# Hybrid retention and attention block on one Trainium2 core: merged branches by token tile at the FFN's start, and four changes of order

## The chip, the cores and the metric

One core of one Trainium2 chip. The metric is the device time in microseconds (us) of one execution, as the median of 3 runs. The engines are named as the profile names them: PE (TensorE, matmuls), DVE (VectorE), ACT (ScalarE), POOL (GpSimd), SP (SyncE, which issues the DMAs).

## What is computed

One decoder block in float32 on 1024 tokens with a model width of 1024:

```
h = rms_norm(x, ln1_g)
proj = h @ w_in + b_in      # ret q, k, v, gate | attn q, k, v | gate_a, gate_b
ry = head_group_norm(retention_chunkwise(rotary(rq), rotary(rk), rv), ret_norm_g)
branch_a = (silu(rg) * ry) @ w_ret_out
ay = sliding_window_sink_attention(rotary(aq), rotary(ak), av, attn_sinks)
branch_b = ay @ w_attn_out
merged = sigmoid(gate_a) * branch_a + sigmoid(gate_b) * branch_b
x = x + merged @ w_out
h2 = rms_norm(x, ln2_g)
x = x + (silu(h2 @ w_ffn_gate) * (h2 @ w_ffn_up)) @ w_ffn_down     # d_ff = 2816
out = rms_norm(x, lnf_g)
```

## The kernel before

Every float32 product is made of three matmuls: both operands are split into a high half (ScalarE casts it, line 128 or 531) and a low half (VectorE subtracts it, line 131 or 532), and hi*hi, hi*lo and lo*hi are summed. `split` does it for weights and `halves` for activations. A product of a 128-column weight block and a 512-token half over 512 input rows is thus 12 matmuls.

The stages follow each other on the one core: LN1 and projections of k and v; attention (lines 284 to 525), whose units u_scores, u_transpose (pT) and u_values run one behind the other while projections and gates fill TensorE; the projection to retention v; the "pairs" (lines 721 to 867), which make retention k, q, gate and the last gates; the retention core with branch B; branch A ("ba", lines 1064 to 1081), which also merges the two and splits the result into the tiles M; the output projection wo (1203 to 1253); the FFN's gate and up products (1379 to 1444); the down projection with the final norm (1476 to 1556).

The retention v, the pairs, the FFN and the down projection use Strassen's scheme in Winograd's form: a 2 x 2 block product by seven products P1 to P7 instead of eight. Their operands are sums and differences of blocks: S2, S1 = xf[2], S3 = A11 minus A21, S4 on the activations, T1 to T4 on the weights. In the FFN, `multiply` uses X[pr]: P6 wants S2 (s12, slices 0 and 1), P5 wants S1 (s12, 2 and 3), P7 S3, P4 A22 (both in s3a) and P3 wants S4 (s4). Products gather in the PSUM banks A (tag "acc"), B (tag "s") and C (tag "t"). `j` counts blocks of weight columns, even ones for the gate and odd ones for up; P6(0) is P6 of block 0.

What sets the order: the pairs and the FFN take their products from a list (`wseq` at 728, `seq` at 1111). `wprep_to(i + 3)` and `prep_to(i + LA)` split the weights in the order of the list, that many ahead. `in_order` holds named engines to the order in which the program is written: VectorE, ScalarE and GpSimd in the pairs (848), VectorE and ScalarE from the last tile of wo to the FFN's first products (`late`, 1234). TensorE there is placed by the scheduler. An engine works its instructions off one after the other.

Around the change:
- T3 = wv[12+k] minus wv[4+k], four subtractions on GpSimd at unit 24 of attention (520 to 524).
- `wprep_to` (737): after P1 and P2 of a block are split, GpSimd makes T1 to T4 for it by `gsub` (751 to 755); T2 lies in a tile of the pool wp, in memory that vacc had.
- wo, second half (nh = 1): for each token tile, LN2's row hx (1243 to 1246), then `columns(t - 1)` (1174), which transposes a tile's hx into the banks h2T (tag "t", two), multiplies by the gain on VectorE (1185) and, from tile 4 on, makes S1, S2 and S3's parts in xf. `early_t` makes T of the first two blocks.
- After wo: s12 and s3a are new tiles in the memory of M, so that S2 is split only then, for three tiles at once (1258, `s2_part`), and for the last tile at 1388; `pieces` splits the others.
- P6 of both j is cut into the first 384 columns and the last 128 (1418 to 1424).
- `stash` (1337) writes a pair's results to DRAM, with four GpSimd instructions (1346).
- The down projection: `dprep` splits the operands of a step three steps ahead (DLA); after a product's 11 steps, its four banks are added to x2 (1543), and P3 and P4 are followed by the final norm's parts (`fin_part`, `fin_rs`, `fin_out`). `abank` (1507) names the banks of dA.

Of the kernel before, what the change touches and what calls it, by code (L numbers as in the profile page):

```python
# [16 lines left out]
P = 128  # L17
# [20 lines left out]
def hybrid_block(ctx: ExitStack, tc: tile.TileContext, x, ln1_g, w_in, b_in, ret_norm_g, w_ret_out,  # L38
# [245 lines left out]
    with tc.tile_pool(name="gt", bufs=1, side="right") as gt, tc.tile_pool(name="w1", bufs=1) as w1:  # L284
# [215 lines left out]
        for i in range(NU + 1):  # L500
            if i % NB == 0 and 0 < i < NU:
                fl.until(3 * (i // NB - 1) + 1)
            if i > 0:
                u_transpose(i - 1)
            if i < NU:
                u_scores(i)
            fl.step((i + 1) * left // (NU + 1) - i * left // (NU + 1))
            if i > 0:
                u_values(i - 1)
                if i % 4 == 0:  # L510
                    g, b, _, Bt, jb, _ = geo(i - 1)
# [212 lines left out]
    for z in range(2):  # L724
# [3 lines left out]
    wseq = [(0, "P2"), (1, "P2"), (0, "P1"), (0, "P6"), (1, "P1"), (0, "P5"), (0, "P7"), (1, "P6"), (0, "P4"), (0, "P3"),  # L728
            (1, "P5"), (1, "P7"), (2, "P1"), (1, "P4"), (1, "P3"), (2, "P2")]
# [444 lines left out]
    def columns(t):  # L1174
# [3 lines left out]
        for q in range(2):  # L1178
            pt = ps("t", 2, f"h2T{t}{q}")
# [3 lines left out]
            o = xf[:, 2 * half + q, :, c]  # L1183
            g = bcol[:, LB + 4 * q:LB + 4 * q + 4].rearrange("p (k o) -> p k o", o=1).to_broadcast([P, 4, P])
# [13 lines left out]
    def s2_part(c):  # L1198
        halves(xf[:, 0, :, c], s12[:, 0, :, c], s12[:, 1, :, c])

    for t in range(NB):
        nc.sync.dma_start(x2[:, t, :], x[t * P:t * P + P, :])
    for nh in range(2):
# [20 lines left out]
        for t in range(NB):  # L1224
            pt = acc(f"wo{nh}{t}")
            for k in range(8):
                hi, lo = ws[k // 2]
                mh = M[k // 4][:, 2 * (k % 4), t * P:t * P + P]
                ml = M[k // 4][:, 2 * (k % 4) + 1, t * P:t * P + P]
# [10 lines left out]
            if nh == 1:  # L1240
# [17 lines left out]
    s2_part(slice(0, 3 * P))  # L1258
# [3 lines left out]
    for pr, (t_, q) in {"P1": (a1, 0), "P2": (a1, 2), "P6": (s12, 0), "P5": (s12, 2), "P7": (s3a, 0),  # L1262
                        "P4": (s3a, 2)}.items():
# [28 lines left out]
    def evict(j, pr, pt):  # L1292
# [88 lines left out]
    early = []  # L1381
    for i, (j, pr) in enumerate(seq):
        if i < 2:
            early.append((j, pr, multiply(j, pr)))
            continue
        if i == 2:
            columns(NB - 1)
            s2_part(slice(3 * P, 512))
# [29 lines left out]
        if pr == "P6" and j < 2:  # L1418

            multiply(j, pr, slice(0, 3 * P))  # L1420
            if j == 1:
                for e in range(2):
                    evict(e, pr, multiply(e, pr, slice(3 * P, 512)))
            continue
        pt = multiply(j, pr)
        if j == NJ - 1:
# [8 lines left out]
            elif pr == "P4":  # L1435
# [4 lines left out]
            elif pr == "P3":  # L1440
# [66 lines left out]
    abank = [acc("dA0"), acc("dA1"), acc("dA2"), ps("pv", 1, "dA3")]  # L1507
    nprep = 0
    fins = []
    nc.sync.dma_start(gf, lnf_g.rearrange("(o d) -> o d", o=1).partition_broadcast(P).rearrange("p o d -> p (o d)"))  # L1510
    DLA = 3
    for pi, pr in enumerate(ORDER):
# [14 lines left out]
        for f in range(cut):  # L1527
# [3 lines left out]
            for tt in range(4):  # L1531
                mms(f, tt)
        while nprep < min(len(steps), pi * NP + NP):
            dprep(nprep)
            nprep += 1
        for tt in range(4):
            for f in range(cut, NP):
                mms(f, tt)
            half, z = {"P1": (0, 0), "P5": (1, 1), "P6": (0, 1), "P2": (0, 0), "P7": (1, 1), "P4": (1, 0),
                       "P3": (0, 1)}[pr]  # L1540
            t = 4 * half + tt
            xv = x2[:, t, z * 512:z * 512 + 512]
            nc.vector.tensor_tensor(out=xv, in0=banks[tt], in1=xv, op=ALU.add)
            if pr == "P5":
                xv = x2[:, tt, 512:1024]
                nc.vector.tensor_tensor(out=xv, in0=banks[tt], in1=xv, op=ALU.add)
            if pr == "P2":
                fin_part(t, 0)
            elif pr == "P7":
                fin_part(t, 1)  # L1550
            elif pr in ("P3", "P4"):
                if fins:
                    fin_out(*fins.pop())
                fin_part(t, z, banks[tt])
                fins.append(fin_rs(t))
# [53 lines left out]
```

## Time and profile before

| | |
|---|---|
| runs, median (lowest to highest) | 1601.73 us (1599.96 to 1602.07), 3 runs |
| the profiled execution | 1603.2 us, span 1601.4 us |
| mean granted TensorE clock | 0.994 of full |
| busy in the span | PE 1577.1 us (98%), DVE 995.7 (62%), ACT 717.2 (45%), POOL 370.1 (23%) |

The span runs from the first to the last instruction; the profiled execution's own time is 1.8 us longer. A busy TensorE may still run at the lower of its two clocks: the granted clock (PEclk) tells. In a row of a timeline, the first number is the start and the second the time to the end of the last of the xN instructions; matmuls overlap, so times of products are read from start to start. The time in brackets is the idle time before the row, with what ended it.

### The profile page before, as it was taken

To read this page: it belongs to the slowest core of one execution; us is meant where nothing else is said; L and a number is where in the kernel's file an instruction comes from. 1 tells how busy PE (TensorE), PEld (TensorE's weight loads), DVE (VectorE), ACT (ScalarE), POOL (GpSimd) and SP (SyncE) were. 2 spreads that over 40 slices of the span, in tenths; PEclk is the share of its full clock that TensorE was granted. 3 is DMA by queue.
4 is the path that set the end of the run, shared out by engine and by line. 5 is a ranking of instruction groups with operands and counts; after the bars stand their busy time and mean duration, and the time that the engine had idled before them with its cause. 6 is when DMAs were issued, how large, how long until landed. Compare 5 with 4: busy or idle time off the path is not lost.

```text
span 1601.4 us, 20912 instructions
## 1 busy us (share of the span) xinstructions
PE 1577.1 (98%) x7507; PEld 1312.6 (82%) x7507; DVE 995.7 (62%) x1767; ACT 717.2 (45%) x1434; POOL 370.1 (23%) x312
## 2 busy tenths in 40 slices
PE   9999999999999999999999999999999999999997
PEld 8887877888878888888888887888888888788886
DVE  6459978677656663878553368444444444678656
ACT  5258877844233333544221255333333333344444
POOL 2000020000044441000000012556655555200001
PEclk9999999999999999999999999999999999999999
DMA  6564655440465455654545102333333333863332
GB/s 197 162 172 126 199 178 159 144 139 34 137 200 151 139 160 187 231 183 159 181 149 183 53 0 67 99 106 105 107 109 107 99 109 109 294 230 88 98 110 114
DMA packets 148886, 223.13 MB, mean 139 GB/s; under 512 B 9195, under 2 KB 81709, under 8 KB 147246
## 3 DMA queue, kind: packets, MB, share of 16 engines
q1 hardware_dynamic: 148782, 221.80, 42.8%
q8 instruction: 59, 0.97, 0.2%
q14 instruction: 45, 0.37, 0.1%
HBM read 149.67 MB, written 67.37 MB: 136 GB/s over the span
## 4 chain that ended last, share of the span: by engine, by line
PE 85%; ACT 6%; DVE 6%; issue 1%; DMA 1%; POOL 1%; POOLq 0%; SPq 0%; ACTq 0%; DVEq 0%
PE fA L1288 15%; PE fB L1288 7%; PE wA L814 7%; PE dA L1523 6%; PE dxP L1523 5%; PE fC L1288 4%; PE wB L814 3%; PE va L659 3%; ACT sc L439 2%; PE vP L659 2%; PE wo L1232 2%; PE wo L1230 2%; PE acc_ba L155 2%; PE acc_ba L157 2%; PE wo L1231 2%; PE acc_ba L156 2%
## 5 line engine op out<-in xcount | busy, mean ns | idle before, releaser
L1523 PE MATMUL dA<-dwP,daP 128*128 128x512 f32 x528 | 121.5, 390 | 2.4 <-DVE dwP L131 2.3
L1523 PEld LDWEIGHTS dA<-dwP,daP 128*128 128x128 f32 x528 | 98.8, 188 | 24.2 <-DVE dwP L131 3.3
L1523 PE MATMUL dxP<-dwP,daP 128*128 128x512 f32 x396 | 90.2, 389 | 0.0
L1523 PEld LDWEIGHTS dxP<-dwP,daP 128*128 128x128 f32 x396 | 74.3, 188 | 15.4
L1346 POOL TENSOR_TENSOR xf<-xf 128x512 f32<-128x512 f32 x44 | 67.7, 1538 | 37.5 <-issue 31.0
L424 POOL COPY sc<-nsink 128x4 f32<-128x4 f32 x32 | 14.4, 452 | 265.1 <-PE pT L457 158.9
L156 PE MATMUL acc_g<-h,wh_g 128*128 128x512 f32 x192 | 75.3, 392 | 0.0
L157 PE MATMUL acc_g<-h,wl_g 128*128 128x512 f32 x192 | 75.2, 392 | 0.0
L155 PE MATMUL acc_g<-h,wh_g 128*128 128x512 f32 x192 | 75.2, 392 | 0.0
L439 ACT ACTIVATE sc<-sc,nm 128x257 f32<-128x257 f32 (+1 forms) x128 | 62.5, 491 | 25.1 <-DVE nm L436 24.9
L1299 POOL TENSOR_TENSOR xf<-xf 128x512 f32<-128x512 f32 x33 | 48.5, 1471 | 56.4 <-DVE xf L1304 37.7
L1309 ACT COPY xf<-fA 128x512 f32<-128x512 f32 x44 | 25.8, 586 | 76.6 <-PE fA L1288 76.6
L436 DVE CUSTOM_DVE_ANT_0 sc<-s,amask,nsink 128x256 f32<-128x256 f32 (+1 forms) x128 | 53.9, 461 | 9.4 <-PE s L433 9.1
L131 DVE TENSOR_TENSOR dwP<-wd,dwP 128x512 fp32r<-128x512 f32 x77 | 53.6, 698 | 4.7 <-ACT dwP L128 4.7
L1468 POOL TENSOR_TENSOR rs_f<-tot,mhalf 128x1 f32<-128x1 f32 x8 | 7.9, 992 | 196.1 <-DVE tot L1465 196.1
L128 ACT CAST dwP<-wd 128x512 fp32r<-128x512 f32 x77 | 47.3, 616 | 10.1 <-PE dA L1523 8.2
L155 PE MATMUL acc_bb<-ay,wh_bb 128*128 128x512 f32 x128 | 50.9, 399 | 0.0
L156 PE MATMUL acc_bb<-ay,wh_bb 128*128 128x512 f32 x128 | 50.3, 393 | 0.0
L156 PE MATMUL aq<-h,wh_aq 128*128 128x512 f32 x128 | 50.2, 392 | 0.0
L155 PE MATMUL aq<-h,wh_aq 128*128 128x512 f32 x128 | 50.1, 391 | 0.0
L157 PE MATMUL aq<-h,wl_aq 128*128 128x512 f32 x128 | 50.0, 392 | 0.0
L157 PE MATMUL acc_bb<-ay,wl_bb 128*128 128x512 f32 x128 | 50.0, 391 | 0.0
(798 smaller groups left out, 4410.6 us busy)
## 6 DMA issues: line engine op xcount, KB each, us to landing
act_d<-xf SPq DMA_DIRECT2D x77, 256.0 KB, 2.1
daP<-act_d SPq DMA_DIRECT2D x21, 512.0 KB
q_d<-stg SPq DMA_DIRECT2D x8, 1024.0 KB
q<-q_d SPq DMA_DIRECT2D x32, 256.0 KB, 6.1
ay_d<-q SPq DMA_DIRECT2D x8, 1024.0 KB
ay<-ay_d SPq DMA_DIRECT2D x4, 2048.0 KB, 13.9
wr_daP<-act_d SPq DMA_DIRECT2D x14, 512.0 KB, 3.6
wr_g<-in_w_in SPq DMA_DIRECT2D x12, 512.0 KB, 4.9
```

The costliest lines, as they stand in the source:

```text
L131: nc.vector.tensor_tensor(out=lo, in0=raw, in1=f32(hi), op=ALU.subtract)
L155: nc.tensor.matmul(pt, hi[:, k, :], xh, start=(k == 0), stop=False)
L156: nc.tensor.matmul(pt, hi[:, k, :], xl, start=False, stop=False)
L157: nc.tensor.matmul(pt, lo[:, k, :], xh, start=False, stop=(k == 7))
L436: nc.vector.tensor_tensor_reduce(out=sc[:, j, 0:nk], in0=pt[:, jj * 256:jj * 256 + nk], in1=mk, scale=1.0, scalar=nsink[:, 4 * g + j:4 * g ...
L439: nc.scalar.activation(sc[:, j, 0:nk + 1], sc[:, j, 0:nk + 1], AF.Exp, scale=-1.0, bias=nm[:, j:j + 1], accum_out=den[:, j:j + 1])
L659: nc.tensor.matmul(vbanks[pr][tt], x_[:, c], w[:, u, :], start=(fresh and k + z == 0), stop=(k == 3 and z == 2), skip_group_check=not fresh)
L814: nc.tensor.matmul(pt, o[:, w, k, :], v, start=(first and k + z == 0), stop=(k == 3 and z == 2), skip_group_check=not first)
L1288: nc.tensor.matmul(pt[:, c], o[:, w, k, :], v[:, c], start=(first and k + z == 0), stop=(k == 3 and z == 2), skip_group_check=not first)
L1299: nc.gpsimd.tensor_tensor(out=dst[q], in0=dst[q], in1=sg[q], op=ALU.mult)
L1346: nc.gpsimd.tensor_tensor(out=o, in0=a, in1=b, op=op)
L1523: nc.tensor.matmul(banks[tt], a[:, u, c], w[:, v, :], start=(fresh and f + z == 0), stop=(f == NP - 1 and z == 2), skip_group_check=not fresh)
```

## The change

Five edits:
- **Start of the FFN.** M is laid out by token tiles (`mview`), so that s12 and s3a can be views of M's memory, each part of which is free as soon as wo has read its tile. S2 (`s2_part`) is split for tiles 4 to 6 and A22 (`a22_part`) for tiles 4 and 5 within the wo loop, each one tile behind; `early_t` comes two tiles sooner. h2T uses the banks "s"; for tiles 6 and 7, ScalarE evicts the second half in four instructions. P6 of j = 1 is no longer cut. P7 and P4 swap places in s3a. TensorE's order is pinned to the program's for the first 16 entries of `seq`.
- **The pairs' first order.** P1 of block 1 and P5 of block 0 come ahead of P6 of block 0.
- **T3 on VectorE**, one subtraction at each of units 25, 27, 29 and 31.
- **The FFN's last block** ends with P7, P3, P4; its stash follows P4; the banks of dA are taken in another order.
- **The down projection**: P3's four results are put off, one behind each of the steps 1 to 4 of P4.

Core of the diff:

```diff
@@ attention
-            if i == 3 * NB:
-                for k in range(4):
-                    nc.gpsimd.tensor_tensor(out=wv[:, 4 + k, :], in0=wv[:, 12 + k, :], in1=wv[:, 4 + k, :],
-                                            op=ALU.subtract)
+            if i > 3 * NB and i % 2:
+                k = (i - 3 * NB) // 2
+                nc.vector.tensor_tensor(out=wv[:, 4 + k, :], in0=wv[:, 12 + k, :], in1=wv[:, 4 + k, :],
+                                        op=ALU.subtract)
@@ pairs
-    wseq = [(0, "P2"), (1, "P2"), (0, "P1"), (0, "P6"), (1, "P1"), (0, "P5"), (0, "P7"), (1, "P6"), (0, "P4"), (0, "P3"),
-            (1, "P5"), (1, "P7"), (2, "P1"), (1, "P4"), (1, "P3"), (2, "P2")]
+    wseq = [(0, "P2"), (1, "P2"), (0, "P1"), (1, "P1"), (0, "P5"), (0, "P6"), (1, "P5"), (0, "P7"), (1, "P6"), (0, "P4"),
+            (0, "P3"), (1, "P7"), (2, "P1"), (1, "P4"), (1, "P3"), (2, "P2")]
@@ branch A and wo
+    def mview(k, t, z):
+        return M[k // 4][:, t, (2 * (k % 4) + z) * P:(2 * (k % 4) + z) * P + P]
...
-                halves(s, M[n // 4][:, 2 * (n % 4), c], M[n // 4][:, 2 * (n % 4) + 1, c])
+                s = s.rearrange("p (t s) -> p t s", s=P)
+                halves(s, *(mview(n, slice(4 * half, 4 * half + 4), z) for z in range(2)))
...
-            pt = ps("t", 2, f"h2T{t}{q}")
+            pt = ps("s", 2, f"h2T{t}{q}")
...
+            if q and t > 5:
+                for k in range(4):
+                    nc.scalar.activation(o[:, k], pt[:, k * P:(k + 1) * P], AF.Copy,
+                                         scale=bcol[:, LB + 4 + k:LB + 5 + k])
+                continue
...
+                if t == NB - 1:
+                    release()
+                    columns(t - 1)
                 nc.scalar.activation(hx, x2[:, t, :], AF.Copy, scale=r)
                 hxs[t] = hx
-                if t > 0:
+                if 0 < t < NB - 1:
                     columns(t - 1)
-                if t in (4, 5):
-                    early_t(t - 4, 2)
+                if t in (2, 3):
+                    early_t(t - 2, 2)
+                if t > 4:
+                    s2_part(t - 1)
+                if 4 < t < NB - 1:
+                    a22_part(t - 1)
...
-    s12 = act.tile([P, 4, 4, 512], F32R, tag="B", name="s12")
-    s3a = act.tile([P, 4, 4, 512], F32R, tag="B", name="s3a")
+    s12, s3a = (m.rearrange("p (q a) (b c) -> p q (a b) c", q=4, b=2) for m in M)
@@ FFN
-        seq += [(j, "P6"), (j, "P5"), (j, "P7")] + ([(j + 1, "P1")] if j + 1 < NJ else []) + [(j, "P4"), (j, "P3")]
-        seq += [(j + 1, "P2")] if j + 1 < NJ else []
+        seq += [(j, "P6"), (j, "P5"), (j, "P7")]
+        seq += [(j + 1, "P1"), (j, "P4"), (j, "P3"), (j + 1, "P2")] if j + 1 < NJ else [(j, "P3"), (j, "P4")]
...
+        if up and pr == ("P3" if j < NJ - 1 else "P4"):
+            stash(j // 2)
...
+    first = in_order(nc.tensor.engine)
+    first.__enter__()
     for i, (j, pr) in enumerate(seq):
+        if i == 16:
+            first.__exit__(None, None, None)
...
-            multiply(j, pr, slice(0, 3 * P))
-            if j == 1:
-                for e in range(2):
-                    evict(e, pr, multiply(e, pr, slice(3 * P, 512)))
+            if j == 0:
+                multiply(j, pr, slice(0, 3 * P))
+            else:
+                pt = multiply(j, pr)
+                evict(0, pr, multiply(0, pr, slice(3 * P, 512)))
+                evict(1, pr, pt)
@@ down projection
-    abank = [acc("dA0"), acc("dA1"), acc("dA2"), ps("pv", 1, "dA3")]
+    abank = [acc("dA0"), acc("dA1"), ps("pv", 1, "dA2"), acc("dA3")]
...
             for tt in range(4):
                 mms(f, tt)
+            if f > 0 and later:
+                result(*later.pop(0))
...
+            if pr == "P3":
+                later.append((pr, tt, banks[tt]))
+            else:
+                result(pr, tt, banks[tt])
```

Three places in the engines' orders. TensorE at the start of the FFN, from the transposes of the last token tile (h2T71) on; fC, fA, fB are the banks with j, t_0P6 the split weights of P6 for j = 0. Before:

```order
L1182 MATMUL h2T71_8902<-ident_81,hx_8832 128x128 x4
L1288 MATMUL fC0_8955<-a1_8447,t_0P2_8826 128x512 x12
L1288 MATMUL fC1_8970<-a1_8447,t_1P2_8828 128x512 x12
L1288 MATMUL fA0_8870<-s12_8859,t_0P6_8856 128x384 x12
L1288 MATMUL fA1_8883<-s12_8859,t_1P6_8867 128x384 x12
L1288 MATMUL fA0_8870<-s12_8859,t_0P6_8856 128x128 x12
L1288 MATMUL fA1_8883<-s12_8859,t_1P6_8867 128x128 x12
L1288 MATMUL fB0_9035<-s12_8859,t_0P5_8927 128x512 x12
L1288 MATMUL fB1_9055<-s12_8859,t_1P5_8930 128x512 x12
L1288 MATMUL fA0_8870<-s3a_8860,t_0P7_8939 128x512 x12
```

and now:

```order
L1188 MATMUL h2T71_8911<-ident_81,hx_8840 128x128 x4
L1309 MATMUL fC0_8967<-a1_8447,t_0P2_8834 128x512 x12
L1309 MATMUL fC1_8982<-a1_8447,t_1P2_8836 128x512 x12
L1309 MATMUL fA0_8879<-m0_7577,t_0P6_8869 128x384 x12
L1309 MATMUL fA1_8892<-m0_7577,t_1P6_8876 128x512 x12
L1309 MATMUL fA0_8879<-m0_7577,t_0P6_8869 128x128 x12
L1309 MATMUL fB0_9035<-m0_7577,t_0P5_8939 128x512 x12
L1309 MATMUL fB1_9055<-m0_7577,t_1P5_8942 128x512 x12
L1309 MATMUL fA0_8879<-m1_7874,t_0P7_8951 128x512 x12
L1309 MATMUL fA0_8879<-m1_7874,t_0P4_8959 128x512 x12
```

P6 of j = 1 is one run of 512 columns, the activations come from M's memory (m0, m1), and P4 of j = 0 follows its P7 directly.

ScalarE at the start of the pairs; w0P6 is the split weight of P6 for block 0, wt2_0 its T2, made by GpSimd, and p10 the kept P1. Before:

```order
L128 CAST w1P2_4394<-wp11_3847 128x512
L128 CAST w0P1_4397<-wr_wp00_3842 128x512
L128 CAST w0P6_4418<-wt2_0_4400 128x512
L128 CAST w1P1_4434<-wr_wp10_3846 128x512
L819 COPY p10_4455<-wA0_4442 128x512
L128 CAST w0P5_4462<-wr_wp00_3842 128x512
```

and now:

```order
L128 CAST w1P2_4394<-wp11_3847 128x512
L128 CAST w0P1_4397<-wr_wp00_3842 128x512
L128 CAST w1P1_4418<-wr_wp10_3846 128x512
L128 CAST w0P5_4439<-wr_wp00_3842 128x512
L819 COPY p10_4455<-wA0_4442 128x512
L128 CAST w0P6_4462<-wt2_0_4400 128x512
```

The cast of w0P6 stands behind those of w1P1 and w0P5, whose raw weights don't come from GpSimd.

VectorE in the down projection, from P3 to P4; dwP42 and daP42 are the operands of P4's step 2, dxP30 to dxP33 P3's four banks. Before:

```order
L1543 TENSOR_TENSOR x2_8175<-dxP32_13021,x2_8175 128x512
L1473 TENSOR_SCALAR x2_8175<-wd22_11822,rs_f_13248 128x512
L1461 TENSOR_TENSOR wd22_11822<-x2_8175,gf_11858 128x512
L1543 TENSOR_TENSOR x2_8175<-dxP33_13022,x2_8175 128x512
L1465 TENSOR_SCALAR tot_13256<-sq_11859 128x1
L1461 TENSOR_TENSOR wd22_11822<-x2_8175,gf_11858 128x512
L1473 TENSOR_SCALAR x2_8175<-wd22_11822,rs_f_13258 128x512
L131 TENSOR_TENSOR dwP42_13273<-wd21_11854,dwP42_13273 128x512
L131 TENSOR_TENSOR daP43_13290<-wr_daP42_13270,daP43_13290 128x512
```

and now:

```order
L131 TENSOR_TENSOR daP42_13235<-wr_daP42_13233,daP42_13235 128x512
L131 TENSOR_TENSOR dwP42_13236<-wd21_11854,dwP42_13236 128x512
L1541 TENSOR_TENSOR x2_8175<-dxP30_13019,x2_8175 128x512
L1541 TENSOR_TENSOR x2_8175<-dxP31_13020,x2_8175 128x512
L1489 TENSOR_TENSOR wd22_11822<-x2_8175,gf_11858 128x512
L1493 TENSOR_SCALAR tot_13274<-sq_11859 128x1
L131 TENSOR_TENSOR daP43_13253<-wr_daP42_13233,daP43_13253 128x512
L131 TENSOR_TENSOR dwP43_13254<-wd21_11854,dwP43_13254 128x512
L1501 TENSOR_SCALAR x2_8175<-wd22_11822,rs_f_13276 128x512
```

dwP42 stood behind all four of P3's results and now stands ahead of them.

## Rows read from the trace of the kernel before

**Rows 1.** The page: span, and its part 1 (busy us, share, instructions).

```profile
span 1601.4 us, 20912 instructions
...
PE 1577.1 (98%) x7507; PEld 1312.6 (82%) x7507; DVE 995.7 (62%) x1767; ACT 717.2 (45%) x1434; POOL 370.1 (23%) x312
```

**Rows 2.** TensorE's waits: engine, line, releaser: total us, times, longest us.

```profile
PE fC L1288 <- DVE xf L1185: 3.1, 1, 3.1
PE dA L1523 <- DVE dwP L131: 2.3, 2, 1.3
...
PE pT L457 <- DVE sc L447: 2.1, 4, 0.8
PE wA L814 <- DVE w1P L131: 1.6, 1, 1.6
```

**Rows 3.** Timeline of TensorE, 955 to 985 (start, us, instruction, [idle before]).

```profile
958.99 1.03 PE L1182 MATMUL h2T<-ident,hx 128*128 128x128 f32 x8
963.10 5.49 PE L1288 MATMUL fC<-a,t_0P 128*128 128x512 f32 x12 [3.08 <-DVE xf L1185]
...
971.37 2.27 PE L1288 MATMUL fA<-s,t_0P 128*128 128x384 f32 x12
...
978.18 2.96 PE L1288 MATMUL fB<-s,t_0P 128*128 128x512 f32 x12
```

**Rows 4.** Windows, FFN start: us, then busy by engine, PEclk, DMA.

```profile
963.00:969.00 6.00, 5.90 (x14) 4.64 (x15) 5.87 (x10) 3.87 (x6) 0.00 (x0) 0.51 0.01 3
```

**Rows 5.** Timeline of VectorE, 950 to 986.

```profile
953.23 0.68 DVE L1238 SCALAR_TENSOR_TENSOR x<-wo,x 128x512 f32<-128x512 f32 x1
...
960.08 1.76 DVE L532 TENSOR_TENSOR s<-xf,s 128x1536 fp32r<-128x1536 f32 x1 [0.68 <-ACT s L531]
...
962.36 1.28 DVE L1185 TENSOR_TENSOR xf<-h2T,bcol 128x512 f32<-128x512 f32 x2
...
983.93 1.78 DVE L131 TENSOR_TENSOR t_0P<-wrx_f,t_0P 128x512 fp32r<-128x512 f32 x1
```

**Rows 6.** Timeline of ScalarE, 950 to 986.

```profile
957.02 1.15 ACT L1245 ACTIVATE hx<-x,rs_ln 128x1024 f32<-128x1024 f32 x1 [1.92 <-POOL rs_ln L97]
...
958.58 1.47 ACT L531 CAST s<-xf 128x1536 fp32r<-128x1536 f32 x1
```

**Rows 7.** Timeline of TensorE, 438 to 475.

```profile
444.08 2.88 PE L814 MATMUL wA<-h,w0P 128*128 128x512 f32 x12
...
450.03 4.50 PE L814 MATMUL wA<-s,w0P 128*128 128x512 f32 x12
...
456.18 2.88 PE L814 MATMUL wB<-h,w0P 128*128 128x512 f32 x12
...
472.50 2.88 PE L814 MATMUL wA<-s,w1P 128*128 128x512 f32 x12
```

**Rows 8.** Timeline of GpSimd, 436 to 460.

```profile
444.65 1.28 POOL L528 TENSOR_TENSOR wt<-wp,wr_wp 128x512 f32<-128x512 f32 x1 [5.81 <-DMA v_d<-vacc]
```

**Rows 9.** Timeline of ScalarE, 436 to 460.

```profile
445.96 0.62 ACT L128 CAST w0P<-wt 128x512 fp32r<-128x512 f32 x1 [9.22 <-POOL wt L528]
```

**Rows 10.** Timeline of GpSimd, 226 to 247.

```profile
233.04 4.39 POOL L523 TENSOR_TENSOR wv<-wv 128x512 f32<-128x512 f32 x3 [4.87 <-DMA wr_g<-in_w_in]
```

**Rows 11.** Timeline of VectorE, 226 to 247.

```profile
226.04 0.62 DVE L447 TENSOR_SCALAR sc<-sc,rd 128x256 f32<-128x256 f32 x2
...
233.66 2.64 DVE L447 TENSOR_SCALAR sc<-sc,rd 128x256 f32<-128x256 f32 x2
```

**Rows 12.** Timeline of VectorE, 1376 to 1400.

```profile
1384.86 2.37 DVE L131 TENSOR_TENSOR dwP<-wd,dwP 128x512 fp32r<-128x512 f32 x2
```

**Rows 13.** Timeline of VectorE, 1556 to 1602.

```profile
1561.41 1.28 DVE L1543 TENSOR_TENSOR x<-dxP,x 128x512 f32<-128x512 f32 x2
...
1568.99 0.69 DVE L131 TENSOR_TENSOR dwP<-wd,dwP 128x512 fp32r<-128x512 f32 x1
```

**Rows 14.** Timeline of TensorE, 1558 to 1602.

```profile
1569.73 24.38 PE L1523 MATMUL dA<-dwP,daP 128*128 128x512 f32 x106 [1.01 <-DVE dwP L131]
```

More of the change, by code (lines that the diff above doesn't have):

```diff
@@ L1196, in columns, with s2_part, a22_part @@
             return eng.tensor_tensor(out=a12, in0=a12, in1=a11, op=ALU.subtract).ins
-    def s2_part(c):
+    def s2_part(t):
+        c = slice(t % 4 * P, t % 4 * P + P)
         halves(xf[:, 0, :, c], s12[:, 0, :, c], s12[:, 1, :, c])
+    def a22_part(t):
+        c = slice(t % 4 * P, t % 4 * P + P)
+        halves(xf[:, 3, :, c], s3a[:, 0, :, c], s3a[:, 1, :, c])
+    s12, s3a = (m.rearrange("p (q a) (b c) -> p q (a b) c", q=4, b=2) for m in M)
     for t in range(NB):
@@ L1227, in hybrid_block @@
                 hi, lo = ws[k // 2]
-                mh = M[k // 4][:, 2 * (k % 4), t * P:t * P + P]
-                ml = M[k // 4][:, 2 * (k % 4) + 1, t * P:t * P + P]
+                mh, ml = mview(k, t, 0), mview(k, t, 1)
                 nc.tensor.matmul(pt, mh, hi[:, k % 2, :], start=(k == 0), stop=False)
@@ L1244, in hybrid_block @@
                 r = rstd_of(m2, 1, f"ln2_{t}")
+                if t == NB - 1:
+                    release()
+                    columns(t - 1)
                 nc.scalar.activation(hx, x2[:, t, :], AF.Copy, scale=r)
                 hxs[t] = hx
-                if t > 0:
+                if 0 < t < NB - 1:
                     columns(t - 1)
-                if t in (4, 5):
-                    early_t(t - 4, 2)
+                if t in (2, 3):
[4 more added lines that the diff above has]
+                    a22_part(t - 1)
                 if t == NB - 1:
-                    release()
                     prep_to(5)
-    s12 = act.tile([P, 4, 4, 512], F32R, tag="B", name="s12")
-    s3a = act.tile([P, 4, 4, 512], F32R, tag="B", name="s3a")
     s4 = [slot("tw", [2, 512], F32R, f"s4{z}") for z in range(4)]
-    s2_part(slice(0, 3 * P))
     prep_to(6)
     X = {}
-    for pr, (t_, q) in {"P1": (a1, 0), "P2": (a1, 2), "P6": (s12, 0), "P5": (s12, 2), "P7": (s3a, 0),
-                        "P4": (s3a, 2)}.items():
+    for pr, (t_, q) in {"P1": (a1, 0), "P2": (a1, 2), "P6": (s12, 0), "P5": (s12, 2), "P7": (s3a, 2),
+                        "P4": (s3a, 0)}.items():
         X[pr] = [(t_[:, q, k, :], t_[:, q + 1, k, :]) for k in range(4)]
@@ L1329, in evict @@
             total(1, "u2")
-            if up:
-                stash(j // 2)
+        if up and pr == ("P3" if j < NJ - 1 else "P4"):
+            stash(j // 2)
     ORDER = ("P1", "P5", "P6", "P2", "P7", "P3", "P4")
@@ L1387, in hybrid_block @@
             columns(NB - 1)
-            s2_part(slice(3 * P, 512))
             woc.__exit__(None, None, None)
@@ L1394, in hybrid_block @@
                 evict(*e)
+            s2_part(NB - 1)
             early_t(0, 1)
@@ L1407, in hybrid_block @@
                 nc.vector.tensor_tensor(out=xf[:, 0, k], in0=xf[:, 3, k], in1=xf[:, 0, k], op=ALU.subtract)
-            pieces(xf[:, 0], s3a[:, 0], s3a[:, 1])
+            pieces(xf[:, 0], s3a[:, 2], s3a[:, 3])
             prep_to(9)
             early_t(0, 4)
-            pieces(xf[:, 3], s3a[:, 2], s3a[:, 3])
+            a22_part(NB - 2)
+            a22_part(NB - 1)
             prep_to(10)
@@ L1434, in hybrid_block @@
                 wload("12", 0, 4)
-            elif pr == "P4":
+            elif pr == "P3":
                 dload("P1", 0)
@@ L1439, in hybrid_block @@
                 wquarter("22", "B")
-            elif pr == "P3":
+            elif pr == "P4":
                 dload("P1", 4)
@@ L1505, in dprep, with result @@
             sub(b21, b21, b11)
-    abank = [acc("dA0"), acc("dA1"), acc("dA2"), ps("pv", 1, "dA3")]
+    def result(pr, tt, bank):
+        half, z = {"P1": (0, 0), "P5": (1, 1), "P6": (0, 1), "P2": (0, 0), "P7": (1, 1), "P4": (1, 0),
+                   "P3": (0, 1)}[pr]
+        t = 4 * half + tt
+        xv = x2[:, t, z * 512:z * 512 + 512]
+        nc.vector.tensor_tensor(out=xv, in0=bank, in1=xv, op=ALU.add)
+        if pr == "P5":
+            xv = x2[:, tt, 512:1024]
+            nc.vector.tensor_tensor(out=xv, in0=bank, in1=xv, op=ALU.add)
+        if pr == "P2":
+            fin_part(t, 0)
+        elif pr == "P7":
+            fin_part(t, 1)
+        elif pr in ("P3", "P4"):
+            if fins:
+                fin_out(*fins.pop())
+            fin_part(t, z, bank)
+            fins.append(fin_rs(t))
+    abank = [acc("dA0"), acc("dA1"), ps("pv", 1, "dA2"), acc("dA3")]
     nprep = 0
     fins = []
+    later = []
     nc.sync.dma_start(gf, lnf_g.rearrange("(o d) -> o d", o=1).partition_broadcast(P).rearrange("p o d -> p (o d)"))
@@ L1538, in hybrid_block @@
                 mms(f, tt)
[L1539 to L1555, printed above, removed]
+            if pr == "P3":
+                later.append((pr, tt, banks[tt]))
+            else:
+                result(pr, tt, banks[tt])
     fin_out(*fins.pop())
```

## The prediction

> **What bounds the kernel.** I read the page's part 1 first [rows 1]: TensorE is busy for 1577.1 us of the span of 1601.4, so at most 24.3 us can be won by filling its idle time, and what is won must be a TensorE wait, or matmuls that ran at the low clock (a busy share doesn't show these). Next the waits of TensorE [rows 2]: 3.1 us for the first fC product of the FFN, 2.3 us at dA (the down projection, two places), 2.1 us at pT in attention, 1.6 us at wA in the pairs; each ends on a VectorE instruction. Then the timelines around each, where the reader should look at start-to-start times, because matmuls overlap. From 456.18 to 472.50 six products of 12 matmuls are issued [rows 7]: 16.32 / 6 = 2.72 us for a product. That is the price of all products below.
>
> **A, start of the FFN.** The transposes of the last token tile start at 958.99; then TensorE waits 3.08 us and fC starts at 963.10 [rows 3]. VectorE gets to evict these transposes only at 962.36, since the cast of S2 for three tiles (1.47 us on ScalarE [rows 6]) and its low half (1.76 us on VectorE [rows 5]) stand ahead. After the wait the granted clock is 0.51 of full [rows 4], its lower level of 1.2 GHz: from 963.10 to 971.37 two products take 8.27 us instead of 2 x 2.72 = 5.44, a loss of 2.83. P6, cut into 384 and 128 columns for both j, takes 978.18 - 971.37 = 6.81 us; the uncut j=1 now takes 2.72 and j=0 keeps half of 6.81, together 6.12, so 0.69 is won.
> The change makes S2 tile by tile in the wo loop and gives h2T the banks "s", so that fC finds "t" free and needn't wait for the eviction. The wait (3.08), the slow matmuls (2.83) and the cut (0.69) go: **6.6**. What is late next: TensorE's order is pinned, so nothing fills a wait. VectorE has, from the last eviction of wo to the low half that P3(0) wants, 28 instructions of 512 columns and 8 of 1024 in the new order. At 1.28 / 2 = 0.64 and 1.76 x 2/3 = 1.17 us [rows 5] these are 17.9 + 9.4 = 27.3 us. TensorE has ahead of P3(0), from 958.99, the transposes (some 0.8 us), 2 products of fC, 6.12 of P6, 2 of P5, and P7(0), P4(0): 0.8 + 6 x 2.72 + 6.12 = 23.2, so it wants P3(0) at 982.2. VectorE starts on this chain at 953.23 [rows 5] and is there at 980.5 plus its own waits (some 1 us). A margin of 0.7 us; the split at 983.93 took 1.78 [rows 5] beside a GpSimd multiply, which would use it up. The scaled row hx ended at 958.17 [rows 6]; four evictions of 128 columns now stand ahead of it on ScalarE, in the 1.92 us that this engine waited there. I take all of 6.6; bounds 3.3 (half comes back as new waits) and 6.9.
>
> **B, the pairs' first order.** From P1(0) at 444.08 to the product that starts at 472.50, 9 products take 28.42 us [rows 7]; 9 x 2.72 = 24.48, so 3.94 is lost, as a wait (1.6 [rows 2]) and as slow matmuls after it (450.03: 4.50 us for 12 that take 2.88). The cause is a queue: the cast for P6(0) at 445.96 waited 9.22 us [rows 9] for the operand that GpSimd makes, which waited 5.81 us for the store of vacc [rows 8]; the split of P1(1) stands behind this cast, though it needs nothing of it. The new order puts P1(1) and P5(0) ahead of P6(0), on ScalarE, VectorE and TensorE alike. P6(0) is then wanted two products after P1(1): 444.08 + 3 x 2.72 = 452.2, and its operand lands at 445.93 [rows 8], with two splits to run. P5(1), moved up, has the smallest margin: by laying the splits out at 0.62 and 0.64 us I find some 0.3 us. I take **3.8**; bounds 1.6 (only the wait goes) and 3.94.
>
> **C, T3 on VectorE.** While GpSimd made three of these differences (4.39 us [rows 10]), VectorE's two L447 instructions took 2.64 us, against 0.62 for two a little earlier [rows 11]; TensorE waited twice for them, with 0.8 the longest and 2.1 in four waits of this kind [rows 2]. The change takes GpSimd away and gives VectorE four instructions of 512 columns, 4 x 0.64 = 2.56 us, one every second unit, at work that waits for nothing else. The two largest waits go: **1.5**. The bounds are 2.1 (all four go) and a loss of 2.6 (each new instruction stands ahead of one that TensorE waits for). I go by the first, because the stretched 2.02 us lay on the path and the new ones are spread.
> The Trainium skill ("SBUF — State Buffer", Who interferes with whom) says that VectorE and GpSimd share a pair of SBUF ports as an exclusive lock, and that one instruction blocks the other for its whole length. The 2.64 us agree. By this rule GpSimd's whole time would be exposed to VectorE wherever both read SBUF, and the term would be at its upper bound, 2.1, the sum 14.1.
>
> **D, end of the FFN.** The last pair now ends P7, P3, P4, and s4's slots come free one product earlier, so that the first splits of the down projection, which ran at 1384.86 (2.37 us for two [rows 12]) and cost 1.3 us [rows 2], come before. But P4 now holds its bank until VectorE has evicted it, and dA's fourth bank is that one: a new wait of some 0.3 to 1.2 by my layout. I take **0.6**; bounds -0.5 (the bank is later than the splits were) and 1.5.
>
> **E, P3 to P4 in the down projection.** VectorE took P3's four results from 1561.41 on, and the split for P4's third step ran only at 1568.99 [rows 13]; TensorE waited 1.01 for it [rows 14]. With the results one by one behind the splits of P4's steps 1 to 4, VectorE's order has the split ahead of them. Hidden by four steps of 2.72 us each. I take **1.1**, the wait and one issue; bounds 0 and 1.2. The tail is unchanged.
>
> **The sum.** 6.6 + 3.8 + 1.5 + 0.6 + 1.1 = 13.6 us, against the profiled execution's own 1603.2: 1589.6. That execution stands 1.5 above the median of the runs, 1601.73, so the forecast is **1588.1**. About 0.2%, 3.2 us, is what a measurement of this kernel can tell from no change.
>
> **The rivals.**
> 1. *The wait moves.* A's margins of 0.7 us are thinner than my layout: hx of the last tile or P3(0) is late and half of A returns. For it: VectorE is nearly always busy there (5.87 of 6.00 us [rows 4]). Against: the pinned order is the one that the data come in. 1588.1 + 3.3 = 1591.4, chance 0.15.
> 2. *T3 lengthens attention.* C is at its lower bound: 1.5 + 2.6 = 4.1 more, 1592.2, chance 0.12. For: every pT wait is behind VectorE. Against: it replaces a stretch of 2.02 us.
> 3. *The slow matmuls stay without the waits.* The low clock isn't undone by shorter waits, or comes at another place: A's 2.83 and B's 3.94 - 1.6 = 2.34 stay, 5.2 in all: 1593.3, chance 0.06. Against it: both stretches follow a wait directly [rows 3, 7]. The Trainium skill ("TensorE: Matmul & The Clock Gate", Part 1) says that the number of slow matmuls varies from run to run and advises against fitting one in a model; by that the 5.2 would not be in the sum.
> 4. *A doesn't do what it says*: fC is held by something other than the eviction, such as hx: 1588.1 + 6.6 = 1594.7, chance 0.05.
> 5. *Slower.* TensorE's order through the FFN's first 14 products is pinned, and VectorE's chain of 27.3 us is behind it at product after product, with no other product to fill in. As after the one wait of 3.08 us, the clock then stays at its lower level, for 12 products: 12 x 2.72 = 32.6 more, 1588.1 + 32.6 = 1620.7. It decides where VectorE takes over 1.3 times as long as rows say, as it does where GpSimd shares its time (1.78 for 0.64 [rows 5]); but GpSimd has no work there before that split. Chance 0.04.
>
> **How the numbers follow.** The forecast has the other 0.58. Its own bounds sum to 6.9 + 3.94 + 2.1 + 1.5 + 1.2 = 15.6, so 1586.1, and the scatter of the runs (1 us each way) makes the low end 1585. The high end takes in rivals 1 to 4, which end at 1594.7: 1595. Left out are rival 5 and pairs of rivals. Faster by over 0.2% means under 1598.5: the forecast and rivals 1 to 4 with little left over, 0.93; within 0.2% only where three terms fail at once, 0.03; slower 0.04.
>
> **What would show it.** In the profile after: no fC wait in TensorE's list, a clock of 1.00 through the FFN's start, P6 in 6.1 us, and fA's P7(0) some 6.6 us sooner in relation to the last transposes (A); 9 products from P1(0) in 24.5 us (B); L447 at 0.62 for two throughout, pT waits of under 1 us (C); dA waits of under 1 us in all (D, E). It is wrong if pT waits grow, if TensorE waits between P5 and P3 at the FFN's start, or if the low clock shows up behind a wait that wasn't there.

## The result and the profile after

The changed kernel takes 1591.14 us (median of 4 runs, 1591.09 to 1592.21) against 1601.84 (4 runs, 1599.96 to 1602.07): the ratio is 0.9937, with a 95% interval of 0.992 to 0.9955. It is 10.7 us faster; 13.6 were forecast. The profiled execution took 1591.11, its span is 1589.3, 12.1 less than the span of the profile before [rows 1].

The page, part 1, of the kernel after:

```profile
span 1589.3 us, 20900 instructions
...
PE 1571.8 (99%) x7495; PEld 1308.3 (82%) x7495; DVE 995.5 (63%) x1773; ACT 720.2 (45%) x1446; POOL 361.1 (23%) x308
```

TensorE's waits after (engine, line, releaser: us in total, times, longest):

```profile
PE fA L1309 <- ACT xf L1330: 1.5, 2, 0.7
PE pT L457 <- ACT sc L445: 1.2, 3, 0.7
...
PE dA L1572 <- DVE xf L1346: 0.8, 1, 0.8
...
PE pT L457 <- DVE sc L447: 0.6, 2, 0.4
...
PE fB L1309 <- DVE xf L1342: 0.4, 1, 0.4
...
PE wC L814 <- DVE w2P L131: 0.2, 1, 0.2
```

Against [rows 2], fC and the wA wait are gone, dA and pT are down; the first row and the fB row are new, and they are the part that I hadn't seen coming.

A total of waits doesn't tell where the time went. For that, follow the same matmul in both traces and watch how its lead grows:

| the same point in both traces | before | after | lead | so the stretch gave |
|---|---|---|---|---|
| first matmul of aq | 46.80 | 46.14 | 0.66 | the head: 0.66, from loads |
| P1(0) of the pairs | 444.08 | 441.40 | 2.68 | attention (C): 2.02 |
| P7(1) of the pairs | 472.50 | 465.88 | 6.62 | pairs (B): 3.94 |
| last tile's transposes | 958.99 | 952.74 | 6.25 | 0.37 given back, at P2 of block 2 |
| P5(0) of the FFN | 978.18 | 965.23 | 12.95 | fC and P6 (A): 6.70 |
| P2 of block 2 of the FFN | 1003.01 | 992.61 | 10.40 | **2.55 lost** |
| first dx product | 1413.07 | 1402.43 | 10.64 | FFN's end (D): 0.24 |
| last dA matmul | 1593.72 | 1581.78 | 11.94 | down, P3 to P4 (E): 1.30 |

The timeline of TensorE after, from the last transposes on, the counterpart of [rows 3]:

```profile
952.74 1.03 PE L1188 MATMUL h2T<-ident,hx 128*128 128x128 f32 x8
953.53 2.98 PE L1309 MATMUL fC<-a,t_0P 128*128 128x512 f32 x12
956.35 2.88 PE L1309 MATMUL fC<-a,t_1P 128*128 128x512 f32 x12
959.07 2.27 PE L1309 MATMUL fA<-m,t_0P 128*128 128x384 f32 x12
...
970.78 2.88 PE L1309 MATMUL fA<-m,t_0P 128*128 128x512 f32 x12
974.39 3.04 PE L1309 MATMUL fA<-m,t_0P 128*128 128x512 f32 x12 [0.73 <-ACT xf L1330]
977.82 3.02 PE L1309 MATMUL fB<-s,t_0P 128*128 128x512 f32 x12 [0.40 <-DVE xf L1342]
980.68 2.88 PE L1309 MATMUL fA<-m,t_1P 128*128 128x512 f32 x12
984.29 3.04 PE L1309 MATMUL fA<-m,t_1P 128*128 128x512 f32 x12 [0.73 <-ACT xf L1330]
```

fC follows the transposes at once, and two fC products take 5.54 us. But P4(0) at 974.39 comes 3.61 us after P7(0) instead of 2.72: 0.89 lost; P3(0) loses 0.71 (3.43), P4(1) 0.89 (3.61): 2.49 in all. ScalarE after, in the same stretch:

```profile
973.75 0.58 ACT L1330 COPY xf<-fA 128x512 f32<-128x512 f32 x1 [0.75 <-PE fA L1309]
```

ScalarE had been idle for 0.75 us and started the copy of P7(0) as soon as TensorE was done. It isn't late: P7 and P4 sum in the same bank, so P4 can't begin before P7's state is copied out, and the list has P4(0) right behind P7(0). P4(1) loses its 0.89 in the same way.

P3(0) loses its 0.71 in another way. It sums in bank B, and VectorE must first take P5's result out of it (L1342). The copy of P7 that this needs was there at 974.33, but VectorE came to it only at 977.09, behind three splits of weights, the first of them stretched to 1.78 us beside a GpSimd multiply (from 973.30, 2.11 us):

```profile
974.18 1.78 DVE L131 TENSOR_TENSOR t_0P<-wrx_f,t_0P 128x512 fp32r<-128x512 f32 x1
...
977.09 0.68 DVE L1342 TENSOR_TENSOR xf<-fB,xf 128x512 f32<-128x512 f32 x1
```

The clock, counterpart of [rows 4] (window, length, busy by engine, PEclk, DMA): 1.00 through the FFN's start.

```profile
953.00:959.00 6.00, 6.00 (x32) 5.09 (x30) 5.83 (x10) 5.06 (x11) 0.00 (x0) 1.00 0.02 4
959.00:965.00 6.00, 6.00 (x36) 5.45 (x35) 6.00 (x8) 2.28 (x5) 0.00 (x0) 1.00 0.00 0
```

### The profile page after: what moved, and what is told of

Same layout as the page of the kernel before. It is cut to its first block, busy times and chain, and to the rows that moved or that the text cites. A ratio compares the mean times of both kernels' runs of the same rounds, so it can differ in the third digit from the quotient of the medians.

```text
span 1589.3 us, 20900 instructions
## 1 busy us (share of the span) xinstructions
PE 1571.8 (99%) x7495; PEld 1308.3 (82%) x7495; DVE 995.5 (63%) x1773; ACT 720.2 (45%) x1446; POOL 361.1 (23%) x308
## 4 chain that ended last, share of the span: by engine, by line
PE 87%; ACT 5%; DVE 5%; issue 1%; DMA 0%; POOL 0%; POOLq 0%; SPq 0%; ACTq 0%; DVEq 0%
PE fA L1309 14%; PE fB L1309 7%; PE dA L1572 7%; PE wA L814 7%; PE dxP L1572 6%; PE fC L1309 3%; PE wB L814 3%; PE va L659 3%; PE acc_g L155 2%; PE acc_g L156 2%; PE vP L659 2%; PE acc_g L157 2%; ACT sc L439 2%; PE acc_ba L156 2%; PE acc_ba L157 2%; PE acc_ba L155 2%
## 5 line engine op out<-in xcount | busy, mean ns | idle before, releaser
L155 PE MATMUL acc_ba<-yg,wh_ba 128*128 128x512 f32 x128 | 49.9, 390 | 0.0
```

The source lines that it names most:

```text
L155: nc.tensor.matmul(pt, hi[:, k, :], xh, start=(k == 0), stop=False)
```

## The experiments

Each is a change to the changed kernel (1591.14), timed in 4 to 6 runs beside the kernel before. That kernel's median was 1601.76 beside experiments 1, 2 and 4, and 1600.92 and 1600.93 beside the two groups of the others, and the head (up to the first matmul of aq) takes 44.59 to 48.04 us in the profiles: where medians of different groups differ by about 1 us, the stretches in the profiles have to decide.

**1. Is the new wait the pin's?** Edit: `first = in_order(nc.tensor.engine)` and its exit taken out.

> The changed kernel without the pin on TensorE's order at the FFN's start (the scheduler's order: four matmuls of P7(1) between P7(0) and P4(0), four of P1(2) ahead of P4(1)). In the changed kernel TensorE loses 0.89, 0.71 and 0.89 us at P4(0), P3(0) and P4(1), 2.49 together. Theory 1 (a product that follows another on the same bank has to wait for ScalarE's copy of the first, and the pin takes away the matmuls that would stand between): the waits before both P4 go, some 1.6 to 1.8 us, and the time is 1591.1 - 1.7 = 1589.4. Rival (VectorE and ScalarE are late with their chain at this place, as the first rival of the prediction has it): the order makes no difference, 1591.1, and TensorE waits for splits or S4 instead.

Measured: 1591.94 (1591.12 to 1594.79), 0.9941 [0.9929, 0.9954] of before: nothing won. The time that I forecast from theory 1 falls, and what the rival named comes: the same time, and a wait for a split. TensorE's timeline without the pin:

```profile
970.74 2.88 PE L1309 MATMUL fA<-m,t_0P 128*128 128x512 f32 x12
973.46 0.61 PE L1309 MATMUL fA<-m,t_1P 128*128 128x512 f32 x2
976.56 0.73 PE L1309 MATMUL fA<-m,t_1P 128*128 128x512 f32 x2 [2.49 <-DVE t_1P L131]
977.13 2.91 PE L1309 MATMUL fA<-m,t_0P 128*128 128x512 f32 x12
```

The scheduler does put four matmuls of P7(1) between, but VectorE still splits P7(1)'s weights in the list's order, after P4(0)'s and P3(0)'s: one wait of 2.49 us in place of three that lose 2.49 (from the last transposes to P2 of block 2, 39.99 us against 39.87 in the changed kernel). With this list the pin is neither gain nor loss. Whether the list is the cause, the next experiment asks.

**2. The list itself** (the part of the list that differs).

```diff
-    (0, "P7"), (0, "P4"), (0, "P3"), (1, "P7"), (1, "P4"),
+    (0, "P7"), (1, "P7"), (0, "P4"), (0, "P3"), (1, "P4"),
```

> The changed kernel, TensorE still pinned, with P7(1) moved between P7(0) and P4(0) in the FFN's list. Theory 1: a whole product (2.72 us) stands between each P7 and the P4 on its bank, so that all three waits go (0.89, 0.71 and 0.89 us): 1591.1 - 2.4 = 1588.7. Rival (the operands are late): the waits move to the splits of P7(1) and P4(0), 1590.5 to 1592.

Measured: 1588.71 (1588.10 to 1589.13), 0.9917 [0.9903, 0.9931]. Theory 1's time to the digit: 2.4 us less than the changed kernel, with no run of the one within the runs of the other. The list is the cause of the three waits. The experiment doesn't tell the two kinds of wait apart, since with P7(1) between, P3(0) too comes a product later. TensorE, without a gap:

```profile
971.29 2.88 PE L1309 MATMUL fA<-m,t_0P 128*128 128x512 f32 x12
974.01 2.88 PE L1309 MATMUL fA<-m,t_1P 128*128 128x512 f32 x12
976.73 2.88 PE L1309 MATMUL fA<-m,t_0P 128*128 128x512 f32 x12
979.45 2.88 PE L1309 MATMUL fB<-s,t_0P 128*128 128x512 f32 x12
```

**3. The same list without the pin.**

> P7(1) between P7(0) and P4(0), without the pin. Theory (what counts is that the list, the splits and TensorE have the same order; the pin only keeps the scheduler from breaking it, and this list leaves it nothing to fill): the same as with the pin, 1588.7 within 0.4. Rival (the pin is needed in any case, as the 2.49 us wait without it in the old list suggests): 1590 or more.

Measured: 1588.56 (1587.43 to 1590.27): the same. In both profiles TensorE takes the products in the same order and needs 37.08 us from the last transposes to P2 of block 2. With splits and products in one order, the scheduler finds nothing to fill here, and the pin has no effect.

**4. T3 back on GpSimd, and T3 left out** (the first with the lines of before, the second with none).

> The changed kernel with T3 back on GpSimd at unit 24, as before. Attention (from the first matmul of aq to the last of pv) was 2.04 us shorter in the changed kernel's profile. Theory: this is due to T3 alone, so 1591.1 + 2.0 = 1593.1, with VectorE's two L447 instructions at 2.6 us again. Rival (it was the scheduler's other order of TensorE in attention, or loads that came sooner): less than 0.7 us of it comes back, 1591.8 or below.

Measured: 1594.07 (1593.40 to 1595.55), 2.9 above the changed kernel. The waits and VectorE's timeline of this kernel:

```profile
PE pT L457 <- DVE sc L447: 3.1, 4, 1.8
```

```profile
235.25 2.62 DVE L447 TENSOR_SCALAR sc<-sc,rd 128x256 f32<-128x256 f32 x2
...
246.34 0.62 DVE L447 TENSOR_SCALAR sc<-sc,rd 128x256 f32<-128x256 f32 x2
```

2.62 us beside GpSimd's three subtractions (from 233.43, 4.29 us), 0.62 ten us later, as in [rows 11]; with T3 on VectorE all are 0.62 or less. Attention (from the first matmul of aq to P1(0) of the pairs, as in the table) takes 398.49 us in this profile, 3.23 more than in the changed kernel's, where the kernel before took 2.02 more. What is more than 2.02 goes with a longer wait and with the clock: behind the two waits on L447 it falls to its lower level in this execution (timeline of TensorE; window), and in the profile before it didn't.

```profile
236.75 0.41 PE L457 MATMUL pT<-ident,sc 128*128 128x128 f32 x2 [1.77 <-DVE sc L447]
```

```profile
240.00:242.00 2.00, 2.00 (x7) 1.61 (x7) 1.97 (x4) 0.92 (x2) 0.45 (x1) 0.50 0.00 0
```

> The changed kernel with T3 left out altogether (the product P7 of retention v then works with the wrong weights). It asks whether the four instructions on VectorE cost something themselves. Theory: they lie in VectorE's slack, so 1591.1 within 0.4. Rival (each of them, 0.64 us, stands ahead of something that TensorE waits for): up to 2.6 less, 1588.5 to 1590.5.

Measured: 1591.01 (1590.60 to 1591.96). The medians differ by 0.1 us, which is less than the runs scatter. In the profile, attention takes 394.38 us, 0.88 less than in the changed kernel's, and the head 0.43 more, as it varies; in all other profiles with T3 on VectorE, attention takes 395.17 to 395.32. So theory's time came, but not its reason: the four instructions aren't all slack; they, or the order in which the scheduler places the rest with them, cost 0.8 to 0.9 us of attention. C's gain is thus what GpSimd took, 2.9 us between these profiles (397.28 before, 394.38 here), less 0.9.

**5. The pairs' first order as before.**

> The changed kernel with the pairs' first order as before. Theory: the wait on w1P (1.6) and the slow matmuls (2.3) come back, less the 0.37 that the new order loses at P2 of block 2: 1591.1 + 3.6 = 1594.7, with a granted clock of about 0.5 for some 3.4 us after the wait. Rival (the clock's fall isn't tied to the wait): 1592.8, the wait alone.

Measured: 1594.90 (6 runs, 1592.51 to 1597.02). The median is what the theory said, but the runs aren't of one kind. In the profiled one (1592.51) the wait is there, and the clock stays up (timeline; then a window):

```profile
446.43 0.73 PE L814 MATMUL wA<-h,w1P 128*128 128x512 f32 x2 [1.57 <-DVE w1P L131]
447.00 2.89 PE L814 MATMUL wA<-s,w0P 128*128 128x512 f32 x12
```

```profile
446.00:451.00 5.00, 4.57 (x20) 3.81 (x21) 2.29 (x3) 1.07 (x2) 4.47 (x4) 1.00 0.49 129
```

The same wait as before, 1.57, but the 12 matmuls behind it take 2.89 us where [rows 7] has 4.50. So the lower clock follows such a wait in some executions only. The runs with a mean granted clock of 0.996 took 1595.86 to 1597.02, those with 0.997 took 1592.51 to 1593.94; that the slower three had the low clock at this place is likely, but only the profiled run has a trace.

**6. The banks of h2T, and S2's place.** Edit: `ps("t", 2, f"h2T{t}{q}")`.

> The changed kernel with the banks of h2T back on the tag t, which fC needs too. In the changed kernel's profile VectorE and ScalarE have evicted the last transposes at 955.0, and fC starts at 953.5. Theory (of A's 3.08 us wait, 1.6 came from S2's place ahead of the eviction, and the other 1.5 from the shared bank): a wait of 1.5 at fC comes back; if the clock then falls as it did after the 1.6 us in the pairs before, up to 2.8 more: 1592.6 to 1595.4. Rival (the bank is all of A): the wait is 3.1 and with the slow matmuls 5.9 come back, 1597.0. If the clock stays at 1.00, 1592.6.

Measured: 1592.11 (1590.77 to 1592.49), 1.0 more by the medians, though the runs overlap with the changed kernel's. The profile shows a wait of 1.32 us at fC, clock 1.00:

```profile
951.39 1.03 PE L1188 MATMUL h2T<-ident,hx 128*128 128x128 f32 x8
953.74 3.06 PE L1309 MATMUL fC<-a,t_0P 128*128 128x512 f32 x12 [1.32 <-DVE xf L1196]
...
974.67 3.04 PE L1309 MATMUL fA<-m,t_0P 128*128 128x512 f32 x12 [0.73 <-ACT xf L1330]
977.55 2.88 PE L1309 MATMUL fB<-s,t_0P 128*128 128x512 f32 x12
```

From these transposes to P1 of block 2 it takes 35.36 us, 0.93 more than in the changed kernel (34.43, 952.74 to 987.17). The rest of the wait is won back at P3(0), and that tells the two kinds of new wait apart. VectorE takes P5's result out of bank B 24.3 us after the transposes in both; TensorE comes to P4(0) 1.6 us later here, and P3(0) no longer waits, while both P4 still lose 0.89.

The other way round, with `s2_part` for tiles 4 to 6 moved behind the wo loop and h2T on "s":

> The changed kernel with S2 of tiles 4 to 6 split after the wo loop, one tile after the other and ahead of the eviction of the last tile's transposes, as the order was before; h2T keeps the banks s. Theory (the bank alone frees fC; S2's place costs only what it delays): fC starts without a wait, and S2 and what follows come some 1.8 us later on VectorE, which P6 or P5 may wait for: 1591.1 to 1592.9. Rival (S2 tile by tile is what took the wait away): a wait of 1.5 us or more at fC, 1592.6 or above.

Measured: 1592.17 (1590.94 to 1593.54). fC doesn't wait:

```profile
955.29 1.03 PE L1188 MATMUL h2T<-ident,hx 128*128 128x128 f32 x8
956.08 2.98 PE L1309 MATMUL fC<-a,t_0P 128*128 128x512 f32 x12
```

From these transposes to P1 of block 2 it takes 34.43 us, as in the changed kernel. The profiled execution (1593.54, the slowest of the five) lost its time elsewhere: TensorE reaches aq 1.90 us later, and 0.7 lies between the pairs' start and the transposes. Why the median is higher isn't shown. So the bank alone takes the wait away, and S2 tile by tile alone leaves 1.3 of it: VectorE has enough slack behind fC to make S2 late.

**7. P3's results not put off.** Edit: `result(pr, tt, banks[tt])` for every product.

> The changed kernel with P3's four results of the down projection right after P3, as before. Theory: TensorE waits 1.0 us for P4's third split again, 1591.1 + 1.2 = 1592.3. Rival (with the other banks of dA the splits run further ahead, and the wait is hidden): 1591.1.

Measured: 1592.58 (1592.18 to 1594.42), 1.4 more, with the old wait:

```profile
1559.23 21.01 PE L1572 MATMUL dA<-dwP,daP 128*128 128x512 f32 x91 [1.00 <-DVE dwP L131]
```

**8. dA's fourth bank.** Edit, on top of experiment 2:

```diff
-    abank = [acc("dA0"), acc("dA1"), ps("pv", 1, "dA2"), acc("dA3")]
+    abank = [acc("dA0"), acc("dA1"), ps("pv", 1, "dA2"), ps("t", 2, "dA3")]
-    banks = [..., ps("t", 2, f"dx{pr}2"), ps("t", 2, f"dx{pr}3")]
+    banks = [..., ps("t", 2, f"dx{pr}2"), acc(f"dx{pr}3")]
```

> P7(1) moved between P7(0) and P4(0) (1588.7 measured), and the fourth bank of dA taken from the tag t, free since P2 of the last block, in place of P4's own; dx then gets P4's bank as its fourth. Theory of D (the new wait of 0.8 us at dA is P4's bank, which VectorE frees late): that wait goes, 1588.7 - 0.8 = 1587.9. Rival (the first splits of the down projection would be the next to be late): a wait on a split of about the same length takes its place, 1588.5 to 1589.

Measured: 1588.53 (1587.23 to 1588.75): no difference from 1588.71 that can be told, and in both profiles 409.8 us from P2 of block 2 to the first dx product. The rival holds, with a wait of 1.12 us for a split:

```profile
1375.23 24.82 PE L1572 MATMUL dA<-dwP,daP 128*128 128x512 f32 x107 [1.12 <-DVE dwP L131]
```

**9. P6(0) whole, and all parts together.**

> P7(1) between P7(0) and P4(0) (1588.7 measured), and P6(0) multiplied whole as well, where the changed kernel still cuts it at 384 columns. In the changed kernel the low half of S2 for the last tile ends at 957.94, and P6(0) starts at 959.07. Theory: the cut costs 0.7 (12 matmuls of 384 and 12 of 128 columns take 3.4 us against 2.72) and S2 is in time: 1588.7 - 0.7 = 1588.0. Rival (the evictions or P5's operands come too late for a TensorE that is 0.7 sooner): 1588.7.

Measured: 1589.10 (1588.39 to 1589.59) against 1588.71: by the runs, no gain. In its profile the stretch from the last transposes (953.36) to P1 of block 2 (984.43) takes 31.07 us, 0.57 less than in experiment 2's (31.64), and the last kernel below has 31.09. So the stretch is shorter by 0.6, near the forecast of 0.7; in the times this is less than the runs scatter.

For the last kernel, the subtractions that make the weights of P5 are put off in the first four steps of P1:

```diff
         if pr == "P1":
-            sub(b11, b12, b11)
+            if f < 4:
+                put_off.append((b11, b12, b11))
+            else:
+                sub(b11, b12, b11)
+                if put_off:
+                    sub(*put_off.pop(0))
```

> The parts that seem to help together: P7(1) between, P6(0) whole, dA's fourth bank from the tag t, and VectorE's subtractions for the weights of P5 in the first four steps of the down projection put off behind the later steps of P1, since the profile with the other bank showed a wait of 1.1 us for a split there in place of the 0.8 for the bank. Theory: 1588.5 - 0.7 - 1.1 = 1586.7. Rival (GpSimd's stash holds VectorE there, not the subtractions): 1587.8.

Measured: **1586.49** (1585.84 to 1587.04), 0.9907 [0.9894, 0.9921] of before, and 4.65 below the changed kernel. The down projection starts without a wait:

```profile
1368.78 29.18 PE L1569 MATMUL dA<-dwP,daP 128*128 128x512 f32 x128
1397.79 4.47 PE L1569 MATMUL dxP<-dwP,daP 128*128 128x512 f32 x19
```

Thus the bank and the subtractions stood one behind the other: the bank alone (experiment 8) only brings the wait of 1.12 in place of the 0.77, and together they give 1.7 (in the table's manner, the lead over the changed kernel grows from 2.93 at the FFN's block 2 to 4.64 at the first dx product). The subtractions put off alone were not run.

## Why the prediction was right, and where it wasn't

The direction, the places and the range (1585 to 1595) held; the time is 3.0 us above the forecast of 1588.1. In the profiles the terms fall short by 2.3 us in sum, and A alone by 2.4. One of the prediction's own signs of being wrong came there: TensorE waits between P5 and P3 at the FFN's start. Step by step, in the profiles:

- **A**: 6.6 forecast, 6.70 - 2.55 = 4.15 measured. The three parts (wait, slow matmuls, cut) came as worked out, even a little more. What failed is the step "what is late next": I laid out when VectorE's operands come (P3(0), hx, the splits) and found them in time, as they were, but never asked of each product which bank it sums in and who must empty it first. P7's copy ends at 974.33, 0.83 us after P4(0) could have followed (970.78 + 2.72 = 973.50), and in the list P4 stands right there: 0.89 twice. The other 0.71, at P3(0), is lateness of VectorE, as rival 1 had it for P3(0), though at the bank and not at an operand: the split for P3(0) ended at 975.96, when the margin that I had worked out was just used up (952.74 + 23.24 = 975.98), and bank B came behind two more splits, at 977.09. So rival 1 had the size (half of A back), and the mechanism for 0.71 of 2.49.
- **A's cause**: I named both S2's place and the bank. Experiment 6 shows that the bank alone is enough: without it a wait of 1.32 us comes back, without S2's new place none does.
- **B**: 3.8 forecast, 3.94 - 0.37 = 3.57 measured in the profiles. The queue behind GpSimd's operand was the cause, and the new order took it away; the margin at P5(1) held. The 0.37 is lost at P2 of block 2, which the prediction doesn't have.
- **C**: 1.5 forecast, 2.02 between the profiles, 2.9 by experiment 4's medians. Undersized: I counted two waits of 0.8. A third, of 1.23 in the next unit, ended on ScalarE's L445 (so rival 2's "every pT wait is behind VectorE" was a wrong reading), and it went too:

```profile
235.18 0.41 PE L457 MATMUL pT<-ident,sc 128*128 128x128 f32 x2 [0.75 <-DVE sc L447]
236.36 0.87 PE L457 MATMUL pT<-ident,sc 128*128 128x128 f32 x6 [0.77 <-DVE sc L447]
...
245.48 1.06 PE L457 MATMUL pT<-ident,sc 128*128 128x128 f32 x8 [1.23 <-ACT sc L445]
```

  These three make 2.75; new waits of 0.5 in later units take some of it back. Nor was the cost of the four instructions on VectorE nothing, as the term had it: experiment 4 puts it at 0.8 to 0.9. The Trainium skill's lock of the port pair ("SBUF — State Buffer", Who interferes with whom) was read as giving 2.1, and 2.02 is near it; the page has the lock only for VectorE instructions in a two-port mode or with two SBUF inputs, which the prediction's "wherever both read SBUF" leaves out.
- **D**: 0.6 forecast, 0.24 measured: the wait for the split (1.29) went and one for P4's bank (0.77) came, as the step said; that leaves 0.5. The other 0.3 lies behind the wait: up to the first dx product TensorE takes 28.66 us for 123 matmuls (0.78 more than at 2.72 for 12), where before it took 27.48 for 119 (0.5 more). What held these matmuls up wasn't tested.
- **E**: 1.1 forecast, 1.30 in the profiles, 1.4 by experiment 7.

The terms sum to 11.3 in the profiles; with 0.66 from the head, which is chance, and what the tail varies, that is 12.1. Between the medians it is 10.7, since the profile before was itself a dear execution, 1.4 us above its median: it had the low clock at both places. Of the 28 runs of the kernel before that were made beside the experiments, 10 with a mean granted clock of 0.994 or 0.995 (as in the profile) have a median of 1602.5, 12 with 0.997 or 0.998 one of 1600.7, and 6 with 0.996 one of 1600.5. So it is likely that of the low clock's price, 2.83 at fC and 2.3 in the pairs in the profile, only a part is in the median; it isn't shown, as no second execution of the kernel before has a trace. If so, my sum counted twice: the 1.5 us by which the profiled execution stood above the median were in part of A and of B already, and without that step the sum gives 1589.6. Rival 3's sentence from the Trainium skill ("TensorE: Matmul & The Clock Gate", Part 1), that the number of slow matmuls varies from run to run, is said there of a kernel's start; experiment 5 shows it in mid-kernel, with 4.50 and 2.89 us for 12 matmuls behind the same wait.

## What to carry to other kernels

When an engine's order is pinned, walk through it twice: once for the operands, and once for the accumulators; a product that continues in a bank needs another product's length between it and the one whose state is still to be copied out. The splits' order and the products' order must be changed together: freeing one alone only moves the wait (2.49 us for 2.49). And the price of a wait that contains a low clock should be taken from several executions, since one profile may hold all of it or none.

## What was not expected of the hardware

After the same wait of 1.57 us of TensorE, the next 12 matmuls took 4.50 us in one execution (granted clock 0.66 of full from 449 to 454, so in part at 1.2 GHz) and 2.89 us in another (2.4 GHz throughout). Matmuls ran at full clock after 1.32 us (experiment 6) and after 2.49 us (experiment 1), and at 0.50 behind 1.77 and 0.77 us of waits in experiment 4, where the kernel before, with 0.75 and 0.77, kept 1.00. Two VectorE instructions of 128 x 256 in SBUF took 2.62 us beside three GpSimd subtractions and 0.62 without; giving VectorE four instructions more (2.6 us at 0.64 each) in GpSimd's place made attention shorter by 2.0.
